# Where the spill loop stands among the last weight loads: a ceiling of 368 loads until the loop is passed

## Chip, cores and metric

One core of a Trainium2 chip. The metric is the time of the program on the device in microseconds (us), median of several runs. The profile is of one execution.

## What is computed

One decoder layer for 512 tokens of width 1024: a combined projection into a gated linear attention and a block-sparse attention, their merge, cross-attention into 256 memory tokens, and a hierarchical mixture of experts, with a final norm. The change lies in the experts: 32 of them, each token goes to two of the eight experts of its group.

```
def run_block(args):
    e, tok, w = args
    xb = xt[tok]
    hid = jax.nn.silu(xb @ w_gate[e]) * (xb @ w_up[e])
    return (hid @ w_down[e]) * w[:, None].astype(xb.dtype)
...
out = jnp.zeros((T, D), h.dtype).at[buf_t].add(yb.reshape(cap, D).astype(h.dtype))
```

`w_gate[e]` and `w_up[e]` are 1024 x 512, `w_down[e]` is 512 x 1024, all float32: 6 MB for an expert, so some 200 MB pass through the chip for the 32.

## The kernel before

The engines are named PE (matmul), ACT, DVE and POOL (elementwise work), and SP, which issues the DMAs. Each has its own queue of instructions and works it off in program order; semaphores hold an instruction until what it needs is there.

**Experts in pairs.** Every expert has 64 slots (`CAP`) for tokens. The loop over `p` takes experts 2p and 2p+1 together, 16 pairs in all: each holds one half of the 128 rows of a tile. A pair does, in this order on PE: gate and up (`gate_up` into the two tiles `gu_ps`, for k of 0 to 7), then, after ACT and DVE have made `hid` from `gu_ps`, products of the pair before (`c_ps`, by `combine`, which DVE adds to the residual `x`) and the transposes `ht_ps`, and the down products (`down` into the two tiles `y_ps`, one for each half of the 1024 columns). ACT and DVE split `y_ps` into `yh` and `yl`, whose products the next pair does. The last pair leaves the loop ahead of its down products: its `combine` is replaced by `last_products`, half by half, followed by the final norm (`scale`, `finish`), the gain row `gf` and the output DMAs.

**The weight loads.** Each load is one DMA of 512 KB into a buffer `we`: rows for two values of k of gate or up (L940), or 128 rows of down (L946). An expert takes 12, a pair 24: loads 1 to 16 of a pair are gate and up (for each quarter of the rows: gate and up of the first expert, then of the second), 17 to 24 are down. There are 384 in all. `eload(n)` issues loads until n have been issued; `DEPTH = 30` keeps the issue order 30 loads ahead of where PE is in the program. SP issues a load when its buffer is free and the load eight before it has landed (there are eight semaphores for DMAs, `DMAHW0` to `DMAHW7`, used in turn). The buffers come from a pool of 48 in turn.

**The spill loop.** Where an expert gets more than 64 tokens, a device loop (`overflow`, L1265; the loop itself is L1268) does the further blocks. Its count is read from the tile `rt_xi` by every engine (L1266, `TENSOR_LOAD`). Ahead of the loop all five engines meet at a barrier: each reports, POOL gathers, and all are released; behind the loop they meet once more. With this input the count is zero, so that all of them branch past it: nothing of its body is in the profile. The loop is written in the last pair, p = 15, ahead of `gate_up`:

```
if p == NP - 1:
    eload(used + SPILL_AT)
    overflow(*spilled)
eload(used + DEPTH)
```

`used` is 360 there and `SPILL_AT` is 8. But the calls of `eload` in pair 14 ask for up to 336 + 30 + 24 = 390 loads, and so the limit in `eload`, 12 * 32 = 384, is reached in that pair: all loads are in SP's queue ahead of the loop, and the call with `SPILL_AT` finds nothing left to do.

Of the kernel before, what the change touches and what calls it, by code (L numbers as in the profile page):

```python
# [26 lines left out]
NE = 32  # L27
# [43 lines left out]
def block_kernel(ctx, tc, x, mem, g_mem, rel_bias, g_mix, w_in, w_alpha_up, b_alpha, g_gla_head, w_proj_gla,  # L71
# [19 lines left out]
    def blk(name, shape, dt=F32):  # L91
        return bp.tile([P] + list(shape), dt, tag="b", name=name)

    def med(name, shape, dt=F32, parts=P):
        return mp.tile([parts] + list(shape), dt, tag="m", name=name)

    def small(name, shape, dt=F32):
        few = math.prod(shape) <= 8
        return sp.tile([P] + list(shape), dt, tag="few" if few else f"s_{name}", name=name, bufs=NS if few else 1)

    def ps(name, shape, parts=P):
        return pp.tile([parts] + list(shape), F32, tag="p", name=name)

    def cut(b):

        at = [0]

        def take(shape, dt=F32):
            size = math.prod(shape) * mybir.dt.size(dt) // 4
            o, at[0] = at[0], at[0] + size  # L110
            ap = b[:, o:at[0]]
            if dt != F32:
                ap = ap.bitcast(dt)
            return ap.rearrange("p (a b) -> p a b", b=shape[-1]) if len(shape) > 1 else ap

        return take
# [40 lines left out]
    def drain(*gens):  # L157
        for g in gens:
            for _ in g:
                pass  # L160
# [10 lines left out]
    plan, loaded, ready, used = [], [], [], [0]  # L171
# [764 lines left out]
    def load_gate_up(e, to=None):  # L936

        for i, (q, w) in enumerate((q, w) for q in range(4) for w in (w_exp_gate, w_exp_up)):
            b = to[i % len(to)] if to else blk("we", [2, 512])
            SY.dma_start(b, wexp(w, e, 2 * q, 2 * q + 2))  # L940
            yield b
# [6 lines left out]


    blocks = [[] for _ in range(NE)]  # L950
    eloads = [0]

    def load_pairs():
        for p in range(NE // 2):
# [10 lines left out]

    def eload(n):

        while eloads[0] < min(n, 12 * NE):
            next(pair_loads)
            eloads[0] += 1  # L970

# [54 lines left out]
    def tile_hots(oh, rel, t, ns, a=None):  # L1026

        a = med("oha", [ns]) if a is None else a
        V.tensor_scalar(a, jc[:, 0:ns], rel[:, t, 0:1], None, op0=ALU.is_equal)
        V.scalar_tensor_tensor(oh[:, t, :], jc[:, 0:ns], rel[:, t, 1:2], a, op0=ALU.is_equal, op1=ALU.add)  # L1030
# [68 lines left out]
    for t in range(NT):  # L1099
# [31 lines left out]
        if t == 1:  # L1131
            eload(PRE[1])
# [62 lines left out]
    def gather(oh, xT, ns):  # L1195

        for k in range(KD):
            o = ps("g_ps", [ns])
            for t in range(NT):
                for q, src in enumerate((xrh, xrl)):  # L1200
                    mm(o, src[t][:, tcol(k)], oh[:, t, :], t == 0 and q == 0, t == NT - 1 and q == 1)
            S.activation(xT[k], o, AF.Copy, scale=gfeat[:, k:k + 1])
            yield

    def slot_rows(codes, n=P, oa=None):

        ot, oa = med("ot", [T], F32R)[0:n], (med("oa", [T]) if oa is None else oa)[0:n]
        c0, c1 = (cw[0][0:n, i, :] for i in range(2))
        V.tensor_scalar(oa, c0, codes, None, op0=ALU.is_equal)
        V.scalar_tensor_tensor(ot, c1, codes, oa, op0=ALU.is_equal, op1=ALU.add)  # L1210
        ws = small("ws", [2])[0:n]
        for i, c in enumerate((c0, c1)):
            V.scalar_tensor_tensor(oa, c, codes, cw[1][0:n, i, :], op0=ALU.is_equal, op1=ALU.mult,
                                   accum_out=ws[:, i:i + 1])
        V.tensor_tensor(ws[:, 0:1], ws[:, 0:1], ws[:, 1:2], op=ALU.add)
        return ot, ws


    def gate_up(gu, k, xk, ws):

        for q in range(2):
            for x, w, own in zip(xk, ws, halves):
                mm(gu[q][own], x, w[2 * (k // 2) + q][:, k % 2, :], k == 0, k == KD - 1, skip_group_check=True)
# [8 lines left out]
    def hidden_t(hid, n=P):  # L1232
        t_ps = ps("ht_ps", [4, n])
        for a in range(4):
            PE.transpose(t_ps[:, a, :], hid[:, a, :], ident[0:n, 0:n])  # L1235
        hid_t = med("hid_t", [4, n])
        S.activation(hid_t, t_ps, AF.Copy)
        return hid_t
# [26 lines left out]
    def overflow(xi, xb):  # L1265
        n_extra = nc.values_load(xi[0:1, 0:1], min_val=0, max_val=NX - 1,  # L1266
                                 skip_runtime_bounds_check_because="2 T assignments fill fewer than NX whole blocks")
        with tc.For_i(0, n_extra, 1, iteration_sync='staggered') as i:  # L1268
            e = nc.sync.value_load(xi[0:1, bass.ds(i + 1, 1)], min_val=0, max_val=NE - 1)
            base = small("base", [1])  # L1270
            V.tensor_copy(base, xb[:, bass.ds(i, 1)])
            rel = small("relx", [NT, 2])
            V.tensor_scalar(rel, code, base, None, op0=ALU.subtract)
            codes = small("codes", [1])
            V.tensor_tensor(codes, pslot, base, op=ALU.add)
            take, take2 = cut(blk("loop", [D])), cut(blk("loop2", [D]))
            oh, part, oa = blk("oh", [NT, CAP], F32R), take([CAP]), take([T])
            xT, hid = take2([KD, CAP]), take2([4, P])
            xT = [xT[:, k, :] for k in range(KD)]
            for t in range(NT):  # L1280
                tile_hots(oh, rel, t, CAP, part)
            drain(gather(oh, xT, CAP))
            ot, ws = slot_rows(codes[0:CAP], CAP, oa)
            to = [blk("we", [2, 512]) for q in range(4)]
            gu, load = [ps("gu_ps", [512]) for q in range(2)], load_gate_up(bass.ds(e, 1), to)
            for j in range(4):
                w = list(islice(load, 2))
                for k in (2 * j, 2 * j + 1):
                    gate_up(gu, k, xT[k:k + 1], [{2 * j + q: w[q] for q in range(2)}])
            hid_t = hidden_t(hidden(gu, ws, CAP, hid), CAP)  # L1290
            y_ps, load = [ps("y_ps", [512]) for c in range(2)], load_down(bass.ds(e, 1), to)
            for ft in range(4):
                down(y_ps, hid_t, ft, [{8 + ft: next(load)}])
            parts = med("yh", [512], F32R), med("yl", [512], F32R)
            for c in range(2):
                drain(combine(ot, {c: rows_hilo(y_ps[c], CAP, parts)}))
# [5 lines left out]
    for p in range(NP):  # L1302
        w = blocks[2 * p:2 * p + 2]
        used = 24 * p
        if p == NP - 1:
            eload(used + SPILL_AT)
            overflow(*spilled)
        eload(used + DEPTH)
        if p % 2 == 0 and p:
            xT = xT_next  # L1310
        gu = [ps("gu_ps", [512]) for q in range(2)]
        s0 = (p % 2) * P
        for k in range(KD):
            gate_up(gu, k, [xT[k][:, s0 + CAP * i:s0 + CAP * i + CAP] for i in range(2)], w)
            if k % 2:
                eload(used + DEPTH + 2 * (k + 1))
            if p == 0 and k >= BC_AT:
                next(bcast, None)
                if k == BC_AT + 3:
                    slot = slot_rows(sid[:, 0:1])  # L1320
                    oh_next = group_hots(1)
        if p % 2 == 0 and p + 2 < NP:
            xT_next = rows2("xT", KD, 4 * CAP)
            gat = gather(oh_next, xT_next, 4 * CAP)
        if p == NP - 1:
            gf = blk("gf", [D])
            SY.dma_start(gf, bcast_rows(g_final, D))
        hid = hidden(gu, slot[1])
        gs = 4 if p + 2 < NP else 0
        steps(gat, min(gs, 1))  # L1330
        steps(comb, 2 if gs else 4)
        hid_t = hidden_t(hid)
        for i in range(3):
            steps(gat, min(gs, 1))
            steps(comb, 2)
        drain(comb)
        ot = slot[0]
        if p + 1 < NP:
            slot = slot_rows(sid[:, 2 * p + 2:2 * p + 3])
        if p % 2 and p + 3 < NP:  # L1340
            oh_next = group_hots((p + 3) // 2)
        if p >= 2:
            next(spill, None)
        y_ps = [ps("y_ps", [512]) for c in range(2)]
        if p == NP - 1:
            break
        for ft in range(4):
            down(y_ps, hid_t, ft, w)
            eload(used + DEPTH + 16 + 2 * (ft + 1))
        ys = {c: rows_hilo(y_ps[c]) for c in range(2)}  # L1350
        comb = combine(ot, ys)
# [59 lines left out]
SPILL_AT = 8  # L1411
# [40 lines left out]
```

## Time and profile before

| | us |
|---|---|
| median of 3 runs | 1001.63 (1000.63 to 1001.95) |
| profiled execution | 1001.05 |
| its span | 999.2 |
| PE busy | 959.1 (96%) |
| DVE busy | 475.5 (48%) |
| ACT busy | 311.8 (31%) |
| DMA queue of SP, share of 16 DMA engines | 68.6% |
| mean granted clock of PE | 0.986 |

The span is what the profiler saw between the first and the last instruction; the execution takes 1.85 us more. Busy times are of one engine over the whole span. PE's 96% counts pipelined matmuls as busy as long as one is under way, so a stage in which it runs slowly for want of weights can read as busy too; the stage has to be looked at by itself. Rows of the order of time give a start and a duration in us, the engine, its line and its operation, and in brackets how long the engine was idle before it and what ended that. A `q` behind an engine's name marks its queue: registers, branches, semaphores and DMA issues.

### The profile page before, as it was taken

To read this page: it belongs to the slowest core of one execution; us is meant where nothing else is said; L and a number is where in the kernel's file an instruction comes from. 1 tells how busy PE (TensorE), PEld (TensorE's weight loads), DVE (VectorE), ACT (ScalarE), POOL (GpSimd) and SP (SyncE) were. 2 spreads that over 40 slices of the span, in tenths; PEclk is the share of its full clock that TensorE was granted. 3 is DMA by queue.
4 is the path that set the end of the run, shared out by engine and by line. 5 is a ranking of instruction groups with operands and counts; after the bars stand their busy time and mean duration, and the time that the engine had idled before them with its cause. 6 is when DMAs were issued, how large, how long until landed. Compare 5 with 4: busy or idle time off the path is not lost. (4 is left out here: it accounts for less than half of the span.)

```text
span 999.2 us, 13897 instructions
## 1 busy us (share of the span) xinstructions
PE 959.1 (96%) x5305; PEld 642.0 (64%) x5305; DVE 475.5 (48%) x1048; ACT 311.8 (31%) x631; POOL 33.4 (3%) x46
## 2 busy tenths in 40 slices
PE   9999999999999999999999999999999999999475
PEld 7889779887888888898844455555444555543122
DVE  6343863445556845467741445444243545322305
ACT  5442643455546434455331111111111111110003
POOL 3200010000000000000000000000000000000003
PEclk9999999999999999999999999999999999999878
DMA  9512346222143505383689999999999999999942
GB/s 300 153 43 64 66 71 181 57 70 85 64 163 130 195 19 146 115 296 126 253 316 376 410 409 409 409 408 409 410 409 409 410 408 409 409 409 410 409 190 85
DMA packets 117161, 252.52 MB, mean 253 GB/s; under 512 B 10310, under 2 KB 61795, under 8 KB 117092
## 3 DMA queue, kind: packets, MB, share of 16 engines
q1 hardware_dynamic: 117092, 251.60, 68.6%
q8 instruction: 43, 0.70, 0.3%
q14 instruction: 26, 0.21, 0.1%
HBM read 247.90 MB, written 3.67 MB: 252 GB/s over the span
## 5 line engine op out<-in xcount | busy, mean ns | idle before, releaser
L136 PE MATMUL gu_ps<-we,xT 128*64 128x512 f32 x1024 | 228.1, 598 | 22.5 <-PEq L1268 21.2
L136 PEld LDWEIGHTS gu_ps<-we,xT 128*64 128x64 f32 x1024 | 75.3, 138 | 169.3 <-issue 157.4
L213 DVE TENSOR_TENSOR wlo<-wraw,whi 128x1024 fp32r<-128x1024 f32 (+1 forms) x71 | 86.4, 1236 | 90.1 <-ACT whi L212 89.8
L136 PE MATMUL y_ps<-we,hid_t 128*64 128x512 f32 x512 | 113.6, 595 | 0.3 <-issue 0.3
L1229 DVE SCALAR_TENSOR_TENSOR hid<-hid,ws,gu_ps 128x512 f32<-128x512 f32 x16 | 12.0, 747 | 211.1 <-PE gu_ps L136 211.1
L1262 DVE TENSOR_TENSOR x<-c_ps,x 128x512 f32<-128x512 f32 x120 | 76.7, 685 | 38.9 <-PE c_ps L136 38.9
L131 PE MATMUL fo<-hTh,whi 128*128 128x512 f32 x224 | 90.5, 404 | 0.0
L133 PE MATMUL fo<-hTh,wlo 128*128 128x512 f32 x224 | 87.5, 391 | 0.0
L132 PE MATMUL fo<-hTl,whi 128*128 128x512 f32 x224 | 87.4, 390 | 0.0
L136 PEld LDWEIGHTS y_ps<-we,hid_t 128*64 128x64 f32 x512 | 35.7, 137 | 68.9 <-issue 58.1
L1228 ACT ACTIVATE hid<-gu_ps 128x512 f32<-128x512 f32 x16 | 9.6, 597 | 213.7 <-PE gu_ps L136 213.7
L212 ACT ACTIVATE whi<-wraw 128x1024 fp32r<-128x1024 f32 (+2 forms) x73 | 74.5, 1043 | 2.0 <-DMA wraw<-in_w_in_dram 1.9
L136 PE MATMUL g_ps<-oh,xrh 128*128 128x256 f32 x256 | 64.6, 293 | 1.7 <-DVE oh L1030 1.7
L136 PE MATMUL g_ps<-oh,xrl 128*128 128x256 f32 x256 | 61.6, 281 | 0.0
L136 PEld LDWEIGHTS g_ps<-oh,xrh 128*128 128x128 f32 x256 | 47.0, 189 | 14.9 <-PE gu_ps L136 9.7
L133 PE MATMUL ro<-whi,hTl 128*128 128x256 f32 (+1 forms) x192 | 55.3, 288 | 0.8 <-DVE hTl L333 0.8
L132 PE MATMUL ro<-wlo,hTh 128*128 128x256 f32 (+1 forms) x192 | 55.3, 288 | 0.7 <-POOL wlo L213 0.7
L131 PE MATMUL ro<-whi,hTh 128*128 128x256 f32 (+1 forms) x192 | 55.8, 291 | 0.0
L212 ACT ACTIVATE yh<-y_ps 128x512 fp32r<-128x512 f32 x32 | 19.1, 598 | 109.3 <-PE y_ps L136 109.3
L136 PE MATMUL c_ps<-yh,ot 128*128 128x512 f32 x128 | 50.7, 396 | 0.7 <-ACT yh L212 0.7
L136 PE MATMUL c_ps<-yl,ot 128*128 128x512 f32 x128 | 50.7, 396 | 0.2 <-DVE yl L213 0.2
L131 PEld LDWEIGHTS fo<-hTh,whi 128*128 128x128 f32 x224 | 42.0, 188 | 12.0 <-issue 3.9
(320 smaller groups left out, 1545.7 us busy)
## 6 DMA issues: line engine op xcount, KB each, us to landing
we<-in_w_exp_gate_dram SPq DMA_DIRECT2D x128, 512.0 KB, 10.2
we<-in_w_exp_up_dram SPq DMA_DIRECT2D x128, 512.0 KB, 10.2
we<-in_w_exp_down_dram SPq DMA_DIRECT2D x128, 512.0 KB, 10.2
wraw<-in_w_in_dram SPq DMA_DIRECT2D x38, 512.0 KB, 3.9
wraw<-in_w_out_dram SPq DMA_DIRECT2D x8, 512.0 KB, 4.5
wraw<-in_w_ckv_dram SPq DMA_DIRECT2D x8, 512.0 KB, 4.6
wraw<-in_w_proj_gla_dram SPq DMA_DIRECT2D x4, 512.0 KB, 3.9
wraw<-in_w_proj_moba_dram SPq DMA_DIRECT2D x4, 512.0 KB, 4.2
```

The costliest lines, as they stand in the source:

```text
L131: PE.matmul(o, lh, rh, start=first, stop=False)
L132: PE.matmul(o, lh, rl, start=False, stop=False)
L133: PE.matmul(o, ll, rh, start=False, stop=last)
L136: PE.matmul(o, l, r, start=first, stop=last, **kw)
L212: S.activation(hi, src, AF.Copy)
L213: eng.tensor_tensor(lo, src, f(hi), op=ALU.subtract)
L1228: S.activation(row, gu[0][0:n], AF.Silu)
L1229: V.scalar_tensor_tensor(row, row, ws[:, 0:1], gu[1][0:n], op0=ALU.mult, op1=ALU.mult)
L1262: V.tensor_tensor(xs, o, xs, op=ALU.add)
```

## The change

The limit in `eload` becomes a variable: 12 * (32 - 2) + 8 = 368 until the spill loop has been written, 384 after it.

```diff
-    eloads = [0]
+    eloads, elimit = [0], [12 * (NE - 2) + SPILL_AT]
...
-        while eloads[0] < min(n, 12 * NE):
+        while eloads[0] < min(n, elimit[0]):
             next(pair_loads)
             eloads[0] += 1
...
         if p == NP - 1:
-            eload(used + SPILL_AT)
+            eload(elimit[0])
             overflow(*spilled)
+            elimit[0] = 12 * NE
         eload(used + DEPTH)
```

The calls in pair 14 now stop at 368, which are loads 1 to 8 of the last pair. The other 16 (its loads 9 to 24) are written by the first `eload(used + DEPTH)` behind the loop. The tiles of the loop's body now take their buffers from the pool ahead of these 16 and not behind them. PE, ACT, DVE and POOL have the same instructions in the same order as before.

SP's queue at the entry of the loop, before: the last pair's loads 19 to 24 (the number behind `we_` is the buffer's), the read of the count, and the barrier ahead of the branch.

```order
L946 DMA we_7997<-in_w_exp_down_dram 128x1024 [waits DMAHW7_49,PE_49]
L946 DMA we_7999<-in_w_exp_down_dram 128x1024 [waits DMAHW0_49,PE_49]
L946 DMA we_8001<-in_w_exp_down_dram 128x1024 [waits DMAHW1_49,PE_49]
L946 DMA we_8003<-in_w_exp_down_dram 128x1024 [waits DMAHW2_49,PE_49]
L946 DMA we_8061<-in_w_exp_down_dram 128x1024 [waits DMAHW3_49,PE_49]
L946 DMA we_8063<-in_w_exp_down_dram 128x1024 [waits DMAHW4_49,PE_49]
L1266 TENSOR_LOAD rt_xi_6457 [waits DVE_49]
L1268 COMPARE_AND_BRANCH [waits barrier_Pool_Activation_PE_DVE_SP_release]
```

And the same place now: loads 5 to 8 of the last pair stand directly ahead of it.

```order
L940 DMA we_7927<-in_w_exp_gate_dram 128x1024 [waits DMAHW1_49,PE_49]
L940 DMA we_7929<-in_w_exp_up_dram 128x1024 [waits DMAHW2_49,PE_49]
L940 DMA we_7949<-in_w_exp_gate_dram 128x1024 [waits DMAHW3_49,PE_49]
L940 DMA we_7951<-in_w_exp_up_dram 128x1024 [waits DMAHW4_49,PE_49]
L1266 TENSOR_LOAD rt_xi_6457 [waits DVE_49]
L1268 COMPARE_AND_BRANCH [waits barrier_Pool_Activation_PE_DVE_SP_release]
```

Loads 9 to 24 have gone from ahead of the count and the barrier. SP's queue behind the loop, before (the gain row of the final norm, then the outputs):

```order
L1327 DMA gf_8342<-in_g_final_dram 128x1024 [waits barrier_Pool_Activation_PE_DVE_SP_release,DMAHW5_49,PE_49]
L1387 DMA out_0_dram<-xo_8480 128x512 [waits DMAHW6_49,DVE_49]
L1389 DMA out_0_dram<-xg_8427 128x512 [waits DMAHW7_49,Activation_49]
L1387 DMA out_0_dram<-xo_8489 128x512 [waits DMAHW0_49,DVE_49]
L1389 DMA out_0_dram<-xg_8432 128x512 [waits DMAHW1_49,Activation_49]
```

And now, from load 18 of the last pair on:

```order
L946 DMA we_8294<-in_w_exp_down_dram 128x1024 [waits DMAHW6_49,PE_49]
L946 DMA we_8296<-in_w_exp_down_dram 128x1024 [waits DMAHW7_49,PE_49]
L946 DMA we_8298<-in_w_exp_down_dram 128x1024 [waits DMAHW0_49,PE_49]
L946 DMA we_8300<-in_w_exp_down_dram 128x1024 [waits DMAHW1_49,PE_49]
L946 DMA we_8302<-in_w_exp_down_dram 128x1024 [waits DMAHW2_49,PE_49]
L946 DMA we_8304<-in_w_exp_down_dram 128x1024 [waits DMAHW3_49,PE_49]
L946 DMA we_8306<-in_w_exp_down_dram 128x1024 [waits DMAHW4_49,PE_49]
L1328 DMA gf_8342<-in_g_final_dram 128x1024 [waits DMAHW5_49,PE_49]
```

The barrier behind the loop now releases load 9 instead of `gf`, and `gf` follows load 24. Lines behind the loop have moved down by one.

## Prediction

> **What bounds the kernel now.** I read the page first (span, 40 slices), then PE's waits near the loop, the order of time around it, the register and semaphore rows of the loop's line, the DMA landings, and the chain at the end. Of the page:
>
> ```profile
> span 999.2 us, 13897 instructions
> PEclk9999999999999999999999999999999999999878
> DMA  9512346222143505383689999999999999999942
> ```
>
> From the 22nd slice on, all 16 DMA engines are full, to the end of the weights: the expert stage runs at the pace of the weight stream. PE's longest wait in the last tenth of the span, and two stretches around it (us, then busy time of PE, PEld, DVE, ACT, POOL, granted clock, DMA share, GB/s):
>
> ```profile
> PE gu_ps L136 <- PEq L1268: 21.2, 1, 21.2
> 934.70:955.80 21.10, 0.00 (x0) 0.00 (x0) 1.21 (x2) 0.60 (x1) 0.00 (x0) 0.62 1.03 410
> 955.80:971.80 16.00, 15.96 (x65) 5.41 (x65) 0.00 (x0) 0.60 (x1) 0.00 (x0) 0.87 0.34 128
> ```
>
> PE does nothing for 21 us at the spill loop (L1268) while the stream goes on at 410 GB/s; then it has 16 us of matmuls for weights most of which have landed, and the stream has nothing left. What holds it there, in order of time (start, duration):
>
> ```profile
> 921.86 0.33 SPq L940 DMA_DIRECT2D we<-in_w_exp_gate_dram  x1
> 930.80 0.33 SPq L940 DMA_DIRECT2D we<-in_w_exp_up_dram  x1
> 932.88 0.33 SPq L940 DMA_DIRECT2D we<-in_w_exp_gate_dram  x1
> 935.51 0.69 DVE L213 TENSOR_TENSOR yl<-y_ps,yh 128x512 fp32r<-128x512 f32 x1 [0.29 <-ACT yh L212]
> 941.85 0.33 SPq L940 DMA_DIRECT2D we<-in_w_exp_up_dram  x1
> 943.12 9.29 SPq L946 DMA_DIRECT2D we<-in_w_exp_down_dram  x8
> 955.70 0.33 SPq L1327 DMA_DIRECT2D gf<-in_g_final_dram  x1
> 955.84 16.02 PE L136 MATMUL gu_ps<-we,xT 128*64 128x512 f32 x64 [21.15 <-PEq L1268]
> ```
>
> These are the last pair's loads 1 (921.86), 8, 9, 16 and 17 to 24. The loop's line itself, and the read of its count (L1266):
>
> ```profile
> L1266 SPq TENSOR_LOAD <-rt_xi x1: 486/486/486, 952.5 to 952.5; - x1
> L1268 DVEq EVENT_SEMAPHORE  x3: 21/21/21, 936.2 to 936.4; - x3
> L1268 SPq EVENT_SEMAPHORE  x4: 17/17/17, 953.6 to 953.8; - x4
> L1268 POOLq COMPARE_BRANCH  x1: 50/50/50, 954.0 to 954.0; - x1
> L1268 PEldq COMPARE_BRANCH  x1: 403/403/403, 954.3 to 954.3; - x1
> L1268 PEldq EVENT_SEMAPHORE  x1: 51/51/51, 955.6 to 955.6; - x1
> ```
>
> All engines meet at the loop's entry. DVE, the last of the four compute engines, has arrived by 936.4; SP reads the count only at 952.5, when its 24th load is issued, and works off its semaphores until 953.8; the branches follow at once, and gf leaves SP at 955.70. So the 21 us are SP's: 17.4 us from 936.4 to 953.8, and some 2 us of crossing (953.8 to 955.70 on SP, to 955.84 on PE).
>
> **The change part by part.** No instruction is added or removed; 16 DMA issues go past the loop in SP's queue.
>
> *SP's arrival.* After load 8 at 930.80 come 0.33 of issue, 0.49 of count and the 0.8 from 953.0 (952.5 + 0.49) to 953.8: about 932.5. Load 9's wait to 932.88 no longer stands ahead. The last to arrive is then DVE at 936.4, and what it waits for there is real work of pair 14. With the same 2 us of crossing, SP issues again at 938.3 and PE starts at 938.4 instead of 955.84.
>
> *The 16 loads.* Each issue costs SP 0.33 us, 5.3 in all, but what paces them is landing: each waits for the load eight before it. The times from issue to landing, for issues at 930.80, 941.85 and 952.1, and then for all gate and up loads and all down loads of the kernel (shortest, median, longest):
>
> ```profile
> DMA to landing us min/median/max: 11.0/11.0/11.0
> DMA to landing us min/median/max: 10.2/10.2/10.2
> DMA to landing us min/median/max: 10.7/10.7/10.7
> DMA to landing us min/median/max: 4.4/10.2/11.0
> DMA to landing us min/median/max: 3.3/10.2/10.8
> ```
>
> Load 8 lands at 941.8, load 16 at 952.05, load 24 at 962.8. Does the stream break while SP is at the loop? Load 9 was to land at about 943.1 (932.88 + 10.2, and the time at which load 17 could go). Issued at 938.3 it would land between 941.6 and 942.7 even behind an empty queue (3.3 to 4.4 us), before its old time; and load 8 is still on its way until 941.8, so the engines hardly run dry. Loads 10 to 13 may follow at once, since loads 2 to 5 have landed by 938; an issue takes 0.33 us, and in the full stream one load lands every 1.27 (941.85 to 943.12). So SP has caught up by about 941 and the stream keeps its old times. The cost of this term lies between 0 (the stream never gaps) and 4 to 5 us (it starts again from empty, second rival); I take 0, since the shortest landing of either kind gives it. It cannot be below 0: the stream is at 410 GB/s already.
>
> *PE's gate and up for pair 15.* It now runs at the stream's pace, as in pair 14, whose load 16 was issued at 910.33 and landed at 920.54:
>
> ```profile
> 920.55 2.79 PE L136 MATMUL gu_ps<-we,xT 128*64 128x512 f32 x10 [0.20 <-DMA we<-in_w_exp_up_dram]
> 923.26 0.50 PE L136 MATMUL c_ps<-yh,ot 128*128 128x512 f32 x1
> 971.79 0.50 PE L136 MATMUL c_ps<-yh,ot 128*128 128x512 f32 x1
> 976.12 5.37 PE L136 MATMUL y_ps<-we,hid_t 128*64 128x512 f32 x24
> 981.42 0.50 PE L136 MATMUL c_ps<-yh,ot 128*128 128x512 f32 x1
> ```
>
> The first c_ps product comes 2.71 us after that landing. For pair 15: 952.05 + 2.71 = 954.76, against 971.79 before: 17.0 us earlier. PE has 54 of 64 matmuls to do ahead of the last landing, and 13.6 us for them from 938.4; at pair 15's full-clock pace of 0.22 (24 in 5.3 us, from 976.12 to 981.42) they take 11.9. If its first 4.2 us ran at half clock, as they do before (0.87 of the clock over 16 us is 0.13 x 16 / 0.5 = 4.2 us at 0.5), this would be late by 0.3, less than the wait of the next step.
>
> *The down products.* Their first half (16 matmuls) needs loads 17 to 24; its last two need load 24. Without a wait PE would reach these at 976.12 + 14 x 0.221 - 17.0 = 962.2. Load 24 lands at 962.8. So 0.6 us of wait is late next, and the shift that reaches the end is 962.8 - 979.2 = -16.4 us. If load 24 lands after 10.2 instead of 10.7, it is 0.5 better.
>
> *The tail.* From 979.2 on nothing changes order: the chain that ended last runs through y_ps, c_ps, x and the two output loops.
>
> ```profile
> 981.49 2.04 PE c_ps L136 x8
> 986.82 0.51 PE c_ps L136
> 991.47 1.00 POOL rr L1381
> 983.03 5.01 POOL L1375 TENSOR_TENSOR xg<-x,gf 128x512 f32<-128x512 f32 x4 [491.91 <-DVE x L1369]
> ```
>
> gf is cover that must hold: SP issues it when load 17 has landed, at 953.4 instead of 955.70, and POOL needs it at 983.03 - 16.4 = 966.6, 13 us later; with 10.7 it is there at 964.1, so 2.5 us are to spare.
>
> *Sum.* The profiled execution took 1001.05 us (span 999.2 and 1.85 around it): 1001.05 - 16.4 = 984.65. The median of the runs, 1001.63, is 0.58 higher: 985.2.
>
> **Rivals.** *The entry waits for the loads in flight.* If SP had to see load 8 land at the loop, it would leave at 941.8 + 1.9 = 943.7, load 9 would land 3.3 to 4.4 later, at 947.0 to 948.1, and all behind it 3.9 to 5.0 late: 989.1 to 990.2. Against it: before, the loop was crossed at 955.7 with load 24 in flight until 962.8.
>
> *The branch fetches its target slowly.* If the instructions behind the branch had to come through the queue that the loads fill, crossing would take as long as a load, 10.2 us in place of the 0.5 from the branches (954.0 to 954.3) to the next semaphores: SP back at 948.0, load 9 at 952.4 instead of 943.1: 9.3 late, 994.5. The Trainium skill speaks for this kind of cost: "Runtime: NRT & Kernel Launch", section "Instruction fetch mechanics", says that a taken branch out of the small prefetched window has to fetch its target by DMA before the engine goes on. The rows show a taken branch under a DMA share of 1.03 and PE's longest branch record at 0.4 us, so if there is such a fetch, it is short here.
>
> *The loop itself is the price (slower).* If the 21.15 us of PE's idle were a delay of the loop counted from the last arrival, and SP merely hid behind it, SP would leave at 936.4 + 21.15 = 957.55, load 9 would land by 961.95, 18.85 late, with nothing to stream meanwhile: -16.4 + 18.85 = +2.4, or 1004.1. It decides from a crossing of 18.7 us (1.9, the 0.4 to spare, and 16.4). Against it: semaphores of SP, release and branches follow each other within 0.3 us of 953.8.
>
> *No effect.* Something else that ends near 953 would have to release the loop; with the same crossing times the kernel would stay at 1001 to 1002. Nothing else in the order of time ends there.
>
> **How the numbers follow.** A difference under 0.2% (2 us) is about what can't be told from none here. Forecast 0.87; loads in flight 0.06; slow fetch 0.03; loop's own price 0.02; no effect 0.02. Faster 0.96, same 0.02, slower 0.02. The predicted time is 985.2. Down, a load 24 at 10.2 us and the runs' spread (1000.63 to 1001.95) give 983.9; up, a crossing longer by up to 4 us reaches the first rival: 989.2.
>
> **What would show it.** SP's load 9 at about 938.3, behind no 0.9 us wait for a landing for its first few issues; PE's wait at L1268 down from 21.2 to about 3.7; DMA share near 1.0 through 936 to 958; gate and up in pieces released by DMA, the first c_ps at 954.8; a short DMA wait of PE at y_ps near 962; the span at about 982.8. A DMA share that falls between 939 and 944 speaks for the first rival; branch records of many us for the second; PE idle at L1268 still near 20 for the third. I am wrong if the crossing grows by more than 0.4 us, which then passes to the end.

## Result and profile after

| | before | ceiling of 368 |
|---|---|---|
| median of 4 runs, us | 1001.13 (1000.16 to 1001.95) | 985.84 (984.63 to 986.70) |
| profiled execution, us | 1001.05 | 986.70 |
| its span, us | 999.2 | 984.9 |

The ratio is 0.9847 (95% interval 0.983 to 0.9864): 15.3 us less. Measured a second time, the same kernel gave 985.59 against 1001.63, 0.9861 (0.9826 to 0.9897; the interval is wide because one of its runs went at a clock of 0.945 and took 996 us, and a slow run of 1214 us is left out of it).

The page after, and PE's wait at the spill loop:

```profile
span 984.9 us, 13897 instructions
PE gu_ps L136 <- PEq L1268: 3.8, 1, 3.8
```

The wait was 21.2 us. In order of time (start, duration), from the start of pair 14's down products to the first half of the last pair's:

```profile
929.30 7.09 PE L136 MATMUL y_ps<-we,hid_t 128*64 128x512 f32 x32
932.50 0.33 SPq L940 DMA_DIRECT2D we<-in_w_exp_up_dram  x1
937.21 0.69 DVE L213 TENSOR_TENSOR yl<-y_ps,yh 128x512 fp32r<-128x512 f32 x1 [0.29 <-ACT yh L212]
940.03 0.33 SPq L940 DMA_DIRECT2D we<-in_w_exp_gate_dram  x1
940.17 13.85 PE L136 MATMUL gu_ps<-we,xT 128*64 128x512 f32 x54 [3.78 <-PEq L1268]
945.28 9.28 SPq L946 DMA_DIRECT2D we<-in_w_exp_down_dram  x8
954.22 2.79 PE L136 MATMUL gu_ps<-we,xT 128*64 128x512 f32 x10 [0.20 <-DMA we<-in_w_exp_up_dram]
956.94 0.50 PE L136 MATMUL c_ps<-yh,ot 128*128 128x512 f32 x1
961.28 5.92 PE L136 MATMUL y_ps<-we,hid_t 128*64 128x512 f32 x24
965.53 0.60 ACT L212 ACTIVATE yh<-y_ps 128x512 fp32r<-128x512 f32 x1 [5.33 <-PE y_ps L136]
```

Load 8 leaves SP at 932.50, DVE's last work ends at 937.90, load 9 leaves at 940.03 and PE starts the last pair at 940.17. Its last ten matmuls now wait for load 16. The chain that ended last shows the new bound, which was not in it before:

```profile
944.42 9.76 DMA we<-in_w_exp_up_dram
954.22 2.79 PE gu_ps L136 x10
957.01 2.05 PE c_ps L136 x8
```

That is the wait for load 16. One more load is waited for behind it, the last one, 24: its issue, its time to landing, and the row of PEld (the loading of weights into PE) that it releases:

```profile
954.24 0.33 SPq L946 DMA_DIRECT2D we<-in_w_exp_down_dram  x1
DMA to landing us min/median/max: 10.1/10.1/10.1
964.42 0.19 PEld L136 LDWEIGHTS y_ps<-we,hid_t 128*64 128x64 f32 x3 [0.37 <-DMA we<-in_w_exp_down_dram]
```

The two profiled executions don't run in step: pair 14's down products start at 929.30, and before at

```profile
927.60 7.09 PE L136 MATMUL y_ps<-we,hid_t 128*64 128x512 f32 x32
979.85 0.60 ACT L212 ACTIVATE yh<-y_ps 128x512 fp32r<-128x512 f32 x1 [4.82 <-PE y_ps L136]
```

Up to there both programs are the same, and the difference of 1.70 us belongs to the runs. So all that follows is counted from that start, T0. The ACT row is the end of the first half of the last down products: 52.25 after T0 before, 36.23 now, so 16.0 us less. From that row to the end of the span it is 19.35 before (999.2 - 979.85) and 19.37 now.

### The profile page after: what moved, and what is told of

Same layout as the page of the kernel before. It is cut to its first block, busy times and chain, and to the rows that moved or that the text cites. A ratio compares the mean times of both kernels' runs of the same rounds, so it can differ in the third digit from the quotient of the medians.

```text
span 984.9 us, 13897 instructions
## 1 busy us (share of the span) xinstructions
PE 961.6 (98%) x5305; PEld 645.2 (66%) x5305; DVE 475.6 (48%) x1048; ACT 311.6 (32%) x631; POOL 33.4 (3%) x46
```

## Experiments

One theory: the end is set by the stream of weights; the loop is crossed 2 us after the last engine has arrived, SP included; a later crossing costs only as far as it interrupts the stream or holds PE beyond what the stream does. The rivals stand in each expectation. All kernels differ from the changed one in the places shown. Measured, with the medians over runs and the last three columns from the profiled execution, counted from T0:

| kernel | median us | ratio to before | load 24 leaves SP | first down half | end of span |
|---|---|---|---|---|---|
| before | 1001.13 | | 24.49 | 52.25 | 71.60 |
| 364 | 990.26 | 0.9891 (0.986 to 0.9922) | 30.46 | 41.79 | 61.17 |
| 368 | 985.84 | 0.9847 (0.983 to 0.9864) | 24.94 | 36.23 | 55.60 |
| 368, second time | 985.59 | 0.9861 (0.9826 to 0.9897) | 24.86 | 36.14 | 55.58 |
| 370 | 984.62 | 0.9835 (0.9822 to 0.9847) | 24.65 | 35.89 | 55.28 |
| 372 | 985.52 | 0.9834 (0.9813 to 0.9856) | 25.11 | 36.33 | 55.76 |
| 376 | 991.44 | 0.9893 (0.9878 to 0.9907) | 24.99 | 42.50 | 61.83 |
| no loop | 986.18 | 0.9839 (0.9826 to 0.9851) | 24.59 | 35.83 | 55.39 |

In six of the kernels the first half of the down products ends 11.2 to 11.3 us after load 24 has left SP, wherever the loop was crossed: there the landing of the last load sets the end. It is 27.8 us before and 17.5 with 376, where PE comes to these products long after the load has landed. 364 and 372 were measured on another chip than the second 368, 370, 376 and the kernel without a loop (the kernel before took 1001.72 and 1001.63 there).

**The changed kernel again.** No edit.

> The changed kernel once more, to be compared with the others beside it. Theory (the end is set by the weight stream, which lost about 0.5 us at the loop): ratio to before 0.983 to 0.987, load 9 issued 2 us after DVE's last arrival and landing 0.4 to 0.6 us late against pair 14. Rival (the profiled run's 0.5 us were chance): load 9 lands on time in this profile.

Ratio 0.9861. Between load 8 and load 17 SP took 944.21 - 931.53 = 12.68 us, against 12.78 in the first profile and 12.32 before (943.12 - 930.80). Load 17 waits for the landing of load 9, so load 9 is late again: 0.36 us here, 0.46 in the first profile.

**No loop.** The spill loop is left out; with this input its count is zero.

```diff
-            overflow(*spilled)
+
```

> The spill loop is left out altogether (its count is zero with this input), and with it both barriers and the branch; all 384 loads are issued without a stop. Stream theory: PE no longer waits at the loop (3.8 us in the changed kernel), but the end stays bound by the landing of the last load: only 0 to 1 us faster than with 368, so 984.5 to 986. Rival (the loop's remaining wait of PE is still on the path to the end): 2 to 4 us faster than with 368, 982 to 984.

986.18 us (984.5 to 986 expected), no faster than with 368 by the times; from T0 0.4 us faster at the first half of the down products and 0.2 at the end. PE in order of time, and the stream:

```profile
936.43 5.08 PE L136 MATMUL gu_ps<-we,xT 128*64 128x512 f32 x18
942.56 1.08 PE L136 MATMUL gu_ps<-we,xT 128*64 128x512 f32 x4 [1.04 <-DMA we<-in_w_exp_gate_dram]
936.00:944.00 8.00, 6.63 (x28) 1.67 (x26) 1.38 (x2) 1.01 (x2) 0.00 (x0) 1.00 1.03 410
```

PE no longer stops, gets 18 matmuls further, and waits for loads instead. The 3.8 us that PE still waits at the loop with 368 are hidden; the rival (2 to 4 us to be had) falls. Load 17 follows load 8 after 945.14 - 932.72 = 12.42 us here, where nothing holds SP up, so 12.32 is itself good to 0.1 only.

**Ceiling 376.** `SPILL_AT` is 16.

```diff
-SPILL_AT = 8
+SPILL_AT = 16
```

> Ceiling 376: all gate and up loads of the last pair ahead of the loop. Theory (the loop waits for SP's arrival, then 2 us of crossing): load 16 leaves SP 7.5 us after DVE's last arrival with the stream unbroken, the loop is crossed some 7 us later than with 368, PE's wait at it is 10.5 to 11.5 us, PE does gate and up at its own pace (16 us, first 4 at half clock): the end 5 to 6 us later than with 368, so 990 to 992. Rival (any ceiling that leaves loads behind the loop releases it at DVE's arrival): time as with 368, 985 to 986.

991.44 us (990 to 992 expected); from T0 6.2 to 6.3 later than with 368, a little over the 5 to 6 expected. Load 16 left SP 5.4 us behind DVE's last work (942.48 - 937.07), not 7.5. SP's last load ahead of the loop, its first behind it, and PE:

```profile
942.48 0.33 SPq L940 DMA_DIRECT2D we<-in_w_exp_up_dram  x1
946.09 7.70 SPq L946 DMA_DIRECT2D we<-in_w_exp_down_dram  x8
946.23 16.75 PE L136 MATMUL gu_ps<-we,xT 128*64 128x512 f32 x64 [10.67 <-PEq L1268]
```

The loop is crossed 3.6 us behind SP's last issue, of which 2 are the crossing and the rest SP's own way to the barrier, as in the kernel before (952.1 to 955.70). It is SP's arrival that releases the loop once SP is the last; that some loads stand behind the loop is not enough.

**Ceiling 370.** `SPILL_AT` is 10.

> Ceiling 370: two more loads ahead of the loop. SP then arrives at about 0.6 us before DVE's last arrival, so the crossing stays where it is, but two more loads (2.5 us of stream) are in flight during it. Stream theory: the DMA share no longer dips, load 17 is issued 12.3 us after load 8 as in the kernel before (12.8 with a ceiling of 368), the end is 0.2 to 0.5 us earlier than with 368. Rival (the loss lies in the crossing or the branch, not in how much is in flight): same dip, same time as with 368.

984.62 us; from T0 0.25 to 0.34 faster at the first down half and 0.3 at the end, within the range expected but less than the times of runs can show. Load 17 follows load 8 after 943.01 - 930.51 = 12.50 us: better than 12.78 and 12.68, not quite the 12.3 expected, and within 0.1 of the kernel without a loop. The stream while SP is away (us, busy times, clock, DMA share, GB/s), with 368 first:

```profile
938.00:939.00 1.00, 0.00 (x0) 0.00 (x0) 0.00 (x0) 0.00 (x0) 0.00 (x0) 1.00 0.87 348
939.00:940.00 1.00, 0.00 (x0) 0.00 (x0) 0.00 (x0) 0.00 (x0) 0.00 (x0) 0.85 0.66 270
940.00:941.00 1.00, 0.83 (x2) 0.32 (x4) 0.00 (x0) 0.00 (x0) 0.00 (x0) 0.50 0.66 266
941.00:942.00 1.00, 1.00 (x6) 0.36 (x4) 0.00 (x0) 0.00 (x0) 0.00 (x0) 0.50 1.03 307
942.00:943.00 1.00, 1.00 (x6) 0.41 (x4) 0.00 (x0) 0.00 (x0) 0.00 (x0) 0.50 0.93 352
```

and with 370:

```profile
938.00:939.00 1.00, 0.83 (x2) 0.33 (x4) 0.00 (x0) 0.00 (x0) 0.00 (x0) 0.50 0.97 385
939.00:940.00 1.00, 1.00 (x6) 0.37 (x4) 0.00 (x0) 0.00 (x0) 0.00 (x0) 0.50 1.06 340
940.00:941.00 1.00, 1.00 (x6) 0.42 (x4) 0.00 (x0) 0.00 (x0) 0.00 (x0) 0.50 1.06 373
941.00:942.00 1.00, 1.00 (x6) 0.33 (x5) 0.00 (x0) 0.00 (x0) 0.00 (x0) 0.94 0.92 365
```

Against 410 GB/s the first stretch is short by 1.24 us of stream (62 + 140 + 144 + 103 + 58, over 410), the second by 0.43. What is in flight during the crossing makes the difference, with the crossing itself the same (SP issues again 10.73 and 10.71 us after T0). The shortfall is more than the 0.46 and 0.18 us by which load 17 comes late; what makes up for the rest is not shown.

**Ceiling 372.** `SPILL_AT` is 12.

> Ceiling 372. Theory: the stream has no gap, but SP arrives some 2 us after DVE, so the loop is crossed 2 us later than with 368 or 370; PE waits 5.5 to 6 us there, restarts at half clock, and gate and up end 1.4 to 2.3 us behind load 16; 0.6 of it is taken up by the wait for load 24. The end is 0.4 to 1.3 us later than with 368: 986 to 987.5. Rival (more loads ahead of the loop are never worse, as between 368 and 370): same as with 370.

985.52 us (986 to 987.5 expected); 0.44 later than 370 from T0 at the first down half, so about as late as 368 (0.1 to 0.2 later, where 0.4 to 1.3 was expected). SP and PE at the loop, the down products, and load 24:

```profile
937.76 0.33 SPq L940 DMA_DIRECT2D we<-in_w_exp_up_dram  x1
941.36 0.33 SPq L940 DMA_DIRECT2D we<-in_w_exp_gate_dram  x1
941.50 15.94 PE L136 MATMUL gu_ps<-we,xT 128*64 128x512 f32 x64 [5.17 <-PEq L1268]
961.70 5.54 PE L136 MATMUL y_ps<-we,hid_t 128*64 128x512 f32 x24
954.35 0.33 SPq L946 DMA_DIRECT2D we<-in_w_exp_down_dram  x1
```

PE waits 5.17 us at the loop (5.5 to 6 expected), then works 15.94 without a wait for a load, and its down products take 5.54 (5.37 before, when all loads had landed; 5.92 with 368). So PE is later, as expected, and the wait for load 24 that is left is 0.17 us. But the expectation had the stream without a gap, and that failed: load 24 leaves SP 25.11 us after T0, 0.46 later than with 370, and the first down half ends 11.2 behind it as elsewhere. The stream still sets the end here, with PE only 0.17 us behind. Why the stream lost time with more loads ahead of the loop is not settled. The rival (more ahead is never worse) is against the profile, but the difference is too small for the times.

**Ceiling 364.** `SPILL_AT` is 4.

> Ceiling 364: only loads 1 to 4 of the last pair ahead of the loop. Stream theory: DVE's last arrival and the crossing stay, so load 5 leaves SP 10.7 us after the start of pair 14's down products, when load 4 has landed: the queue is empty, the load takes 3.3 to 5.2 us and is 3.6 to 5.5 us late against an unbroken stream; all behind it keep this, and the end is 3 to 5 us later than with 368: 988.5 to 991. Rival (the stream makes up for a gap, since PE has time to spare in the last pair): within 1 us of the kernel with 368.

990.26 us, 5.6 later than with 368 from T0 (3 to 5 expected). The stream passes its gap on to the end; the rival falls. But the gap was larger than worked out. SP's issues 4, 5 and 13, and the time from issue to landing of load 5 and then of load 6:

```profile
925.42 0.33 SPq L940 DMA_DIRECT2D we<-in_w_exp_up_dram  x1
938.05 0.33 SPq L940 DMA_DIRECT2D we<-in_w_exp_gate_dram  x1
943.39 0.60 SPq L940 DMA_DIRECT2D we<-in_w_exp_gate_dram  x1
...
DMA to landing us min/median/max: 3.7/3.7/3.7
DMA to landing us min/median/max: 6.0/6.0/6.0
```

Load 5 lands 3.7 us after its issue, at 941.75, about 4.0 us late against an unbroken stream, within the 3.6 to 5.5 expected. Load 17 leaves SP 21.50 us after T0 (948.83), where it was 15.52 before (943.12): 6.0 late. The other 2 us are lost between, while eight loads are issued into the drained queue:

```profile
940.00:941.00 1.00, 1.00 (x6) 0.41 (x4) 0.00 (x0) 0.00 (x0) 0.00 (x0) 0.50 0.92 373
941.00:942.00 1.00, 1.00 (x5) 0.30 (x4) 0.00 (x0) 0.00 (x0) 0.00 (x0) 0.50 0.96 254
942.00:943.00 1.00, 1.00 (x4) 0.26 (x2) 0.00 (x0) 0.00 (x0) 0.00 (x0) 0.50 0.74 180
943.00:944.00 1.00, 1.00 (x6) 0.39 (x3) 0.00 (x0) 0.00 (x0) 0.00 (x0) 0.73 0.67 246
```

The rate is 180 to 254 GB/s for 3 us, though loads are waiting. By the Trainium skill, "DMA: Bandwidth & Descriptors", section "Anatomy of one DMA — SWDGE (gpsimd) path", a transfer costs about 2.0 us and its bytes at 436 GB/s, an estimate of 3.2 us for 512 KB. Load 5's 3.7 is near it, on the other path of issue; that a refilled queue then runs below its rate is in these rows alone.

## Why the prediction was right

985.2 was forecast and 985.84 measured, inside 983.9 to 989.2.

- *SP's arrival and the crossing.* Load 9 at 938.3 in the time of before is 10.7 after T0; it left at 940.03 - 929.30 = 10.73. From the end of DVE's `yl` it took 2.13 us, 2.1 by the forecast (936.2 to 938.3). That SP's arrival was the cause is shown by the ceilings 372 and 376, which bring the wait back in steps.
- *The stream keeps its times.* This term was mis-sized: 0 was taken, 0.46 measured (load 17, 12.78 us behind load 8 and not 12.32). It was bounded by the landing of one load behind an empty queue, 3.3 to 4.4 us. That was the wrong row: in the 364 kernel one load did land within that bound (3.7 us), but the loads behind it came slower than the stream, and with 368 load 9 itself took 5.2 us (load 17, which waits for it, left at 945.28). The DMA share was to stay near 1.0; it fell to 0.66 from 939 to 941, which the forecast had expected of its first rival alone. The queue needs enough in flight for the whole crossing and for the restart; with two loads more the loss halves or better, though with four more load 24 is late again (372).
- *Gate and up at the stream's pace.* 956.94 - 954.22 = 2.72 us from the start of the last ten matmuls to the first `c_ps`, 2.71 forecast. From T0 this product came 16.55 us earlier than before (971.79 - 927.60 = 44.19, now 27.64), 17.0 forecast; the 0.46 of the stream is the difference.
- *The wait for load 24.* 0.6 forecast; the down products took 5.92 instead of 5.37, so 0.55. Together: -17.0 + 0.46 + 0.55 = -16.0, where -16.4 was forecast. That 0.55 meets 0.6 is luck, since two sizes behind it were off and cancel. Load 24 landed 10.1 us after its issue and not 10.7, at about 964.34; by the forecast's count PE comes to the matmuls that need it at 961.28 + 14 x 0.221 = 964.37, so there would have been no wait. But the forecast had 0.65 us from there to the end of the first half (979.85 - 979.2), and from the landing to the ACT row it was 965.53 - 964.34, about 1.2: what PE still has to do once load 24 is there takes some 0.5 us more than the forecast had. Counted by load 24, its later issue makes 0.45, the shorter landing -0.6 and this step 0.5: together the 0.4 by which -16.4 was missed.
- *The half clock hidden.* PE did restart at half clock (0.50 from 940 to 943), and it cost nothing: PE was at the last ten matmuls 0.20 us ahead of load 16, and with 370 it restarts at 0.50 too and ends within 0.1 us of the kernel without a loop, whose clock stays at 1.00.
- *gf as cover.* It left SP at 955.52, and the POOL work that reads it waited for DVE alone, as before:

```profile
968.74 5.00 POOL L1376 TENSOR_TENSOR xg<-x,gf 128x512 f32<-128x512 f32 x4 [476.16 <-DVE x L1370]
```

- *The rivals.* Loads in flight: load 8 took 11.1 us and landed at 943.6, 3.6 after SP had left the loop; not waited for. Slow fetch behind the branch: from DVE's last work to load 9 it is 2.13 us, count, barriers and branch together. The loop's own price: PE's wait went to 3.8, and without the loop nothing more is won.

What the forecast did not hold apart is the run: the shift of 16.0 us from T0 shows as 14.35 between the two profiled executions and 15.3 between the medians, since the executions start the experts up to 2 us apart.

## What to carry to other kernels

A queue that prefetches far ahead also arrives late at a barrier written behind its prefetch (here 17.4 us behind the last of the others); where engines meet, put behind the meeting what the queue could not have issued by the time the others arrive. The ceiling has an optimum between two costs: enough in flight to feed the DMA engines through the crossing and the restart, and no more than lets the queue arrive with the others. Here 10 of 24 loads were best of the five counts measured; by the profiles 8 and 12 cost a few tenths of a microsecond more, which the times of runs can't tell apart, and 4 and 16 cost 6 us. Once the stream is the bound, waits of the compute engines in that stage are worth nothing until they exceed what the stream holds back.

## What was not expected of the hardware

A drained DMA queue that is refilled by a burst of issues does not come back at once to its rate: 373, 254, 180 and 246 GB/s in the four microseconds from 940 with a ceiling of 364, and in three of the profiles (364 and both of 368) one issue of such a burst held SP for 1.1 to 1.5 us, where the others take 0.33 to 0.7:

```profile
941.88 1.49 SPq L940 DMA_DIRECT2D we<-in_w_exp_gate_dram  x1
```

Why was not settled; no run spaced the issues out.

PE's clock fell after different idle times: before, PE was idle from 934.69 and the slice from 939 to 940 has 0.78 (half clock from about 939.6, 4.9 us idle); after, idle from 936.39 and 0.85 in the same slice (from about 939.7, 3.3 us); with 364, idle from 934.42 and 0.86 from 936 to 937 (from about 936.7, 2.3 us). The Trainium skill, "TensorE: Matmul & The Clock Gate", section "What's actually happening", puts it after at least one idle window of about 3.4 us and says that the windows run freely. The 4.9 us agrees with that and 3.3 is about one window, but 2.3 us falls short of it.

The same instructions reach the expert stage at different times: the first expert load left SP at 424.01 before and at 425.49 after, with nothing changed ahead of it, and over the eight profiled executions at 423.68 to 425.56. That spread is larger than what 368, 370 and 372 differ by, so they could be told apart only from T0, and only by one or two profiles each.
